# A token shift's move of 127 partitions, issued as one of 112 and one of 15

## Chip, core and metric

The kernel runs on one core of one Trainium2 chip. The metric is the device time of one execution in microseconds (us). A core has a tensor engine (PE, with its weight loads shown apart as PEld), VectorE (DVE), ScalarE (ACT), GpSimd (POOL), the queue of SyncE (SP), from which this kernel issues all its transfers, and 16 DMA engines that move the data.

## The reference

Two transformer blocks over 256 tokens of 1024 channels. The first has a feed forward part, a mixer of two branches (an RWKV-7 recurrence and a dilated attention), and a second feed forward part; the second block has two layers of three branches each. What the change touches is the input side of the RWKV-7 branch:

```python
def token_shift(p, mu):
    prev = jnp.pad(p, ((0, 0), (1, 0), (0, 0)))[:, :-1]
    return p + (prev - p) * mu

def rwkv7_time_mix(p, mu, w0, w2, a0, a2, g2, k_k, k_a, r_k, ln_w, ln_b):
    p = token_shift(p.astype(jnp.float32), mu)
    r, k, v, wd, ad, gd = _split_last(
        p, (RWKV_WIDTH, RWKV_WIDTH, RWKV_WIDTH, DECAY_LORA, AAA_LORA, GATE_LORA))
    ...
```

Each token's projection is mixed with that of the token before it; the first token has zeros before it.

## The kernel before

Tokens lie on the 128 partitions, in two tiles of 128. A projection of 512 columns is a product (`gemm`): four loads of weights of 512 KB (two chunks of 128 rows each, `weights`, line 194), for each of them a split into a high part `wh` (ACT, line 201) and a rest `wl` (DVE, line 202), and then three matmuls for each chunk and token tile (lines 213 to 215), 48 matmuls in all. The raw weights have four buffers, the split ones three.

`shift` works on a product's two accumulators. ACT copies them side by side into `pr` (128 partitions, two tiles, n columns). Token t then lies in partition t, and its predecessor one partition above, so the predecessors are brought down by a transfer inside SBUF: line 471 moves `pr[0:127]` to `pv[1:128]`, 127 partitions of 2n numbers each. Line 472 moves one row more, the last token of the first tile to the first partition of the second, and line 470 zeroes the first row. Lines 473 to 475 on DVE form `pr + (pv - pr) * mu`.

`shift` is called seven times: once with 288 columns for the low-rank inputs (`rwkv_lora`; the tiles are named `lp` and `lv` there), and six times with 512 columns, for k, r and v of each of two groups of eight heads (`rwkv_keys`). The first four are emitted one after the other; the three of the second group stand among the steps of the recurrence, the dilated attention, the gates and the rows of the modulation (products `ada` with weights `wa`, line 1103, loaded by line 1099). The string `PLAN` gives that order by hand, a letter a step. Each engine works off its own queue in order: what stands behind line 473 on DVE, as the next `wl`, starts after it, and what stands behind a transfer on SP is issued after it.

Of the kernel before, what the change touches and what calls it, by code (L numbers as in the profile page):

```python
# [17 lines left out]
DRAM = bass.MemoryType.DRAM  # L18

# the steps of other work emitted after each step of the RWKV halves (see first_block)  # L20
# the order in which the RWKV part and the work beside it are emitted, a letter a step (see first_block)
PLAN = "0000rk000rrrraa0000krk0010rgr010ar01r11rgaar1r1aarra1aaa11r1a1ara11rara1r1a1aa"
P = 128
# [16 lines left out]
def shape_constants():  # L40
    """Arrays fixed by the shapes alone: permutations, masks, rotary and Fourier tables."""
    f = np.float32
    i = np.arange(P)
    parts = []
# [6 lines left out]
    same = (i[:, None] // 64) == (i[None, :] // 64)  # L51
# [45 lines left out]
    # real input: cosines of frequencies 0 to 128, sines of 1 to 127  # L97
# [6 lines left out]
class SplitT:  # L104
    """Feature-major activations as exact hi + lo float32r parts, w tokens (256 or 512) to a stream."""
# [10 lines left out]
    def toks(self, kc, t0, n):  # L116
        """n tokens from t0 on, of chunk kc."""
        self.b.need(self, t0, n)
        o = t0 % self.w
        return tuple(x[:, kc % self.m, o:o + n] for x in self.parts[t0 // self.w, kc // self.m])  # L120
# [11 lines left out]
class Builder:  # L132
# [48 lines left out]
    def weights(self, nk, segs, per=2):  # L181
        """The (k chunk, hi, lo) of a column chunk of up to 1024 / per columns, loaded and split per k chunks at a time."""
# [34 lines left out]
    def gemm(self, xT, nk, segs, toks):  # L217
        """One column chunk (<= 512 columns, from the (W, row, col, n) segments) for the given
        (token tile, first column, end column) list; accumulators come back by token tile."""
        self.aside()  # L220
        acc = {}
        for part in self.weights(nk, segs):
            self.products(acc, xT, nk, part, toks)
            self.tick(len(toks))
        return acc

    def gemm_t(self, xT, nk, segs, w):
        """The first w tokens' column chunk, 2**18 / w columns or half as many, with the result's features on the
        partitions: accumulators of one or two chunks of 128 features."""
# [5 lines left out]
        if w == xT.w == 512:  # L235
            turns = [(f, 0, [part]) for part in self.weights(nk, segs) for f in range(nf)]
        else:
            # a bank's accumulations one after the other
            parts = list(self.weights(nk, segs, 4))
            turns = [(f, t0, parts) for f in range(nf) for t0 in range(0, w, 256)]  # L240
# [16 lines left out]
    def gemm_groups(self, xT, nk, segs, groups):  # L257
        """The same with one group of token tiles after the other, each group's accumulators yielded when complete."""
        parts = list(self.weights(nk, segs))
        for toks in groups:  # L260
            acc = {}
            for part in parts:
                self.products(acc, xT, nk, part, toks)
                self.tick(len(toks))
            yield acc
        self.aside()

# [1 line left out]
    @staticmethod  # L269
    def pipeline(items, stages):  # L270
        """Emit the stages of independent items skewed, each stage one item behind the one before; a step per yield."""
# [7 lines left out]
    def rsqrt(self, m, n, name):  # L279
        """1/sqrt(m) for [P, n] positive m: bit-level first guess, three Newton steps."""  # L280
# [29 lines left out]
    def to_split(self, src, n, xT, kc, t):  # L310
        """[128 tokens, n*128] -> feature-major hi/lo at chunk kc."""
        for c in range(0, n, 4):
# [4 lines left out]
            # stay inside one part  # L317
# [15 lines left out]
    def norm_steps(self, xT, t, x, gain, shift):  # L333
        """The normalised tile, split and feature-major in xT, in three steps of which the first needs no TensorE."""
# [15 lines left out]
    def later(self, xT, t, *args):  # L350
        """Begin tile t's norm; its other steps come between the products that follow, or when its result is read."""
# [5 lines left out]
    def tick(self, n):  # L357
        """n of a tile's products with a part of the weights have been emitted."""
# [10 lines left out]
    def ffn(self, X, xT, groups, w_in, w_out, scale, gates, nxt):  # L369
        """X[t] += scale * gates[s] * (silu(h Wg) * (h Wu)) Wo, the sigmoid's half folded into scale; xT holds h.  # L370
        groups: the token tiles in the order that the input comes in and the result goes out. nxt() gives a function
        that is called with a group once its result is complete."""
# [4 lines left out]
        w = xT.w  # L377
# [44 lines left out]
    def normed(self, X, rows, w=256):  # L422
        """An empty SplitT, and the function that fills in a group of token tiles, normalised with their stream's
        (gain, shift)."""
# [7 lines left out]
    def outgoing(self, xT, nk, W, groups, res, done):  # L432
        """The last two column chunks of a residual's update, so that one group of token tiles is complete before the
        other: with two tiles to a group the weights come twice, else the second chunk goes by groups."""
# [30 lines left out]
    def shift(self, acc, n, mu, pr, pv):  # L465
        """pr [P, 2, n] <- token-shifted projection; acc the two accumulators."""
# [4 lines left out]
        nc.sync.dma_start(out=pv[1:P, :, :], in_=pr[0:P - 1, :, :])  # L471
# [37 lines left out]
    def rwkv_keys(self, xT, hh, st):  # L509
        """Eight heads' key, receptance and value projections, shifted by a token; a step of emission per yield."""  # L510
# [7 lines left out]
    def rwkv_prep(self, hh, st):  # L518
        """The operands of their recurrence; a step of emission per yield."""
# [10 lines left out]
        # low-rank decay, in-context rate and gate  # L530
# [16 lines left out]
        # running log-decay inside chunks of 64 tokens  # L547
# [23 lines left out]
        # normalised key, rate-scaled key  # L571
# [32 lines left out]
        # operands by chunk: side of the in-context rates on the chunk's own partitions, keys and values opposite  # L604
# [37 lines left out]
    def rwkv_solve(self, hh, st, yT):  # L642
        """Their recurrence over chunks of 64 tokens, group norm, bonus and gate; a step of emission per yield."""
# [11 lines left out]
        # chunk Gram matrices, transposed: rows the b and k sides, columns a | r  # L655
# [21 lines left out]
        # unit-triangular inverse: 32-blocks by forward substitution, a block's even and odd columns on two partitions  # L677
# [43 lines left out]
        # bonus  # L721
# [8 lines left out]
        def norm(t):  # L730
            """Group norm, bonus and gate of a token tile."""
# [23 lines left out]
        # per chunk: solve, and the chunk's transition and read-out matrices  # L755
# [82 lines left out]
    def dilated(self, xT):  # L838
# [18 lines left out]
        def prep(g):  # L857
# [4 lines left out]
            # per-head normalised q | k, feature-major: [2 heads x 64, (q01, q23, k01, k23), 256 tokens]  # L862
# [23 lines left out]
        def scores(it):  # L886
# [9 lines left out]
            # statistics by (query tile, head of the group, group)  # L896
# [31 lines left out]
        # weight of group g: e^(m_g - M) / sum den_g' e^(m_g' - M)  # L928
# [20 lines left out]
    def gate_chunk(self, xT, W, col, w, bias=None):  # L949
        """tanh(half the gate pre-activation) for 256 columns, features on the partitions, tanh by accumulator."""  # L950
# [12 lines left out]
    def merged(self, w):  # L963
        """The branches' sum, features on the partitions, as slices of 512: one or two chunks of 128 features."""
# [3 lines left out]
    def project(self, yT, nk, W, c0, n, w, gates, M, first):  # L968
        """M (+)= 2 sigmoid(gate) * (y @ W) on the n columns from c0; the slices' indices."""
# [12 lines left out]
    def last_projection(self, yT, nk, W, w, gates, M, first, w_out, groups, res, nxt):  # L982
        """The last branch's projection, column chunk by column chunk; then the residual's update from M @ w_out."""
# [86 lines left out]
    def ada(self, l, wide=True):  # L1070
        """Rows silu(c) @ w_ada + b_ada for the latent and the context condition, left in DRAM."""
# [41 lines left out]
    def ada_apart(self, l):  # L1113
        """The same beside the tensor engine's work, in steps: the products and the sums over a partition's rows on
        VectorE."""
# [52 lines left out]
    def mods(self, l, i, streams):  # L1168
        """(gain, shift) rows: norm_g * (1 + scale), shift."""
# [11 lines left out]
    ORDER = ((2, 3, 0, 1), (3, 2, 1, 0))  # L1181

    def ml_gates(self, xT, W, l):
# [8 lines left out]
        # gates on partitions, tokens (context first) along the row  # L1192
# [10 lines left out]
        # input and forget gates apart, a direction's heads from partition 0 and 32, the backward direction turned round  # L1203
# [10 lines left out]
        # b: running log-forget within a chunk; c = i - b; M: running maximum with the carried one  # L1214
# [31 lines left out]
        # to columns, tokens on partitions; the backward direction's turned back  # L1246
# [24 lines left out]
    def mlstm(self, xT, W, l, outs, yT):  # L1271
# [4 lines left out]
        for h in range(4):  # L1276
# [3 lines left out]
            def product(segs):  # L1280
                """The accumulators by token tile, the first head's by stream as the input comes in."""
# [93 lines left out]
            # half of 1/rms, the sigmoid's other half  # L1375
# [123 lines left out]
    def fourier(self, xT, W, outs, yT):  # L1499
# [6 lines left out]
        for c in range(2):  # L1506
# [5 lines left out]
            for s in sorted({t // 2 for t in outs}):  # L1512
                for g in range(2):
                    # over the tokens: [channel, cosine part 0..128 | sine part 1..127]
# [8 lines left out]
                    # over the channels: even part 0..128 | odd part 1..127 of the result over the token frequencies  # L1523
# [15 lines left out]
    def second_layer(self, l, X, xT, nxt):  # L1539
        """X: residual tiles; the context's are loaded late and kept in the first layer only."""  # L1540
# [47 lines left out]
    def context(self):  # L1588
        """The context's part of the first layer's input, in steps."""
# [78 lines left out]
```

## Time and profile before

| what | us |
|---|---|
| time, median of three runs | 3113.98 |
| lowest, highest run | 3113.44, 3116.66 |
| span of the profiled execution | 3110.0 |
| PE busy in the span | 2907.0 (93%) |
| DVE busy | 1774.7 (57%) |
| ACT busy | 1178.5 (38%) |

The profile is of one execution; its span runs from the first to the last instruction. Busy time is that of instructions at work, and a busy tensor engine isn't one at its peak. "Idle before" is the time that an engine stood still ahead of an instruction, with what ended it. The granted clock is given as a share of the tensor engine's full 2.4 GHz. The chain of waits is followed back from the last instruction, at each step to what released it. The shifts lie between 224 and 510 us of the span.

### The profile page before, as it was taken

What the parts mean: (1) busy time and instruction counts of PE and PEld (TensorE: products, weight loads), DVE (VectorE), ACT (ScalarE), POOL (GpSimd) and SP (SyncE); (2) the same over time, 40 slices, a digit from 0 to 9 for tenths busy, and PEclk for the clock granted to TensorE, in tenths of its full rate; (3) what the DMA queues carried; (4) which work ended last, traced back from release to release, by engine and by line L of the source; (5) the groups of instructions that cost most, each with busy time, mean ns of one, the idle gap of its engine ahead of it and who ended that gap; (6) DMA issues with size and microseconds to landing.
All of it is one profiled execution on the core that took longest, in us unless ns stands there. A gap on an engine that the chain in (4) does not pass through costs nothing.

```text
span 3110.0 us, 42442 instructions
## 1 busy us (share of the span) xinstructions
PE 2907.0 (93%) x16704; PEld 2435.7 (78%) x16704; DVE 1774.7 (57%) x3036; ACT 1178.5 (38%) x1943; POOL 98.6 (3%) x265
## 2 busy tenths in 40 slices
PE   8994668999899999999999999999999999999998
PEld 7983445667689788898788897878778898789797
DVE  5552563755565545534767337686865455675665
ACT  4442222233344434322553333323244443454443
POOL 1010000000010000000000002000020000000000
PEclk9997787998999999999999999999999999999999
DMA  6653453553655422123124235455542234245564
GB/s 201 189 153 97 142 156 111 155 164 120 199 179 184 135 68 68 55 85 101 48 62 153 75 104 187 145 171 153 161 157 75 89 111 136 81 127 160 178 188 144
DMA packets 291231, 409.57 MB, mean 132 GB/s; under 512 B 30547, under 2 KB 181971, under 8 KB 291032
## 3 DMA queue, kind: packets, MB, share of 16 engines
q1 hardware_dynamic: 291032, 406.86, 42.8%
q8 instruction: 131, 2.15, 0.3%
q14 instruction: 68, 0.56, 0.1%
HBM read 396.98 MB, written 3.24 MB: 129 GB/s over the span
## 4 chain that ended last, share of the span: by engine, by line
PE 77%; DVE 8%; DMA 7%; issue 3%; ACT 3%; POOL 2%; SPq 0%; ACTq 0%; POOLq 0%; DVEq 0%
PE g L214 11%; PE g L215 11%; PE g L213 11%; PE g L250 10%; PE g L248 10%; PE g L249 10%; DMA pv<-pr 2%; DVE wl L202 2%; PE dC L1361 1%; PE tr L316 1%; DMA wa<-in_w_ada_dram 1%; PE ada L1103 1%; DMA wr<-in_w_in_dram 1%; PE I L1337 1%; ACT dae L1458 1%
## 5 line engine op out<-in xcount | busy, mean ns | idle before, releaser
L202 DVE TENSOR_TENSOR wl<-wr,wh 128x1024 fp32r<-128x1024 f32 (+1 forms) x606 | 733.8, 1213 | 718.3 <-ACT wh L201 716.8
L201 ACT CAST wh<-wr 128x1024 fp32r<-128x1024 f32 (+1 forms) x606 | 630.5, 1042 | 1121.6 <-PE g L215 515.1
L214 PE MATMUL g<-wl,xh 128*128 128x512 f32 (+2 forms) x1880 | 736.5, 392 | 32.5 <-DVE wl L202 32.4
L213 PE MATMUL g<-wh,xh 128*128 128x512 f32 (+2 forms) x1880 | 734.9, 394 | 17.5 <-ACT wh L201 12.8
L215 PE MATMUL g<-wh,xl 128*128 128x512 f32 (+2 forms) x1880 | 730.2, 389 | 0.0
L248 PE MATMUL g<-xh,wh 128*128 128x256 f32 (+1 forms) x2352 | 725.4, 309 | 3.6 <-ACT wh L201 3.6
L250 PE MATMUL g<-xh,wl 128*128 128x256 f32 (+1 forms) x2352 | 722.2, 307 | 1.9 <-DVE wl L202 1.9
L249 PE MATMUL g<-xl,wh 128*128 128x256 f32 (+1 forms) x2352 | 721.8, 307 | 0.1
L248 PEld LDWEIGHTS g<-xh,wh 128*128 128x128 f32 x2352 | 451.9, 192 | 32.9 <-issue 4.9
L250 PEld LDWEIGHTS g<-xh,wl 128*128 128x128 f32 x2352 | 451.5, 192 | 31.1 <-issue 7.6
L249 PEld LDWEIGHTS g<-xl,wh 128*128 128x128 f32 x2352 | 451.8, 192 | 26.6 <-issue 7.0
L214 PEld LDWEIGHTS g<-wl,xh 128*128 128x128 f32 x1880 | 361.6, 192 | 111.5 <-DVE wl L202 40.0
L213 PEld LDWEIGHTS g<-wh,xh 128*128 128x128 f32 x1880 | 359.5, 192 | 100.0 <-ACT wh L201 16.8
L215 PEld LDWEIGHTS g<-wh,xl 128*128 128x128 f32 x1880 | 361.1, 192 | 72.8 <-issue 2.9
L1153 DVE SCALAR_TENSOR_TENSOR aa<-wa,cond,aa 128x512 f32<-128x512 f32 x168 | 114.9, 745 | 3.4 <-DMA wa<-in_w_ada_dram 3.4
L303 ACT CAST xh<-tr 128x256 fp32r<-128x256 f32 (+1 forms) x114 | 50.4, 463 | 130.1 <-PE tr L316 116.9
L1103 PE MATMUL ada<-wa,cond 128*2 128x512 f32 x192 | 51.9, 643 | 46.5 <-DMA wa<-in_w_ada_dram 46.3
L1458 ACT ACTIVATE dae<-sc,dast 128x512 f32<-128x512 f32 (+1 forms) x96 | 58.5, 614 | 42.2 <-DVE dast L1456 37.3
L473 DVE TENSOR_TENSOR pv<-pv,pr 128x1024 f32<-128x1024 f32 x6 | 7.4, 1226 | 112.7 <-DMA pv<-pr 112.7
L304 DVE TENSOR_TENSOR xl<-tr,xh 128x256 fp32r<-128x256 f32 (+1 forms) x114 | 57.6, 531 | 21.7 <-ACT xh L303 21.4
L1456 DVE TENSOR_REDUCE dast<-sc 128x1 f32<-128x512 f32 (+1 forms) x96 | 53.8, 596 | 24.1 <-PE sc L1455 23.7
L316 PE MATMUL tr<-ident,hn 128*128 128x128 f32 x160 | 28.3, 312 | 39.1 <-DVE hn L343 19.5
(392 smaller groups left out, 2665.8 us busy)
## 6 DMA issues: line engine op xcount, KB each, us to landing
wr<-in_w_in_dram SPq DMA_DIRECT2D x156, 512.0 KB
wr<-in_ffn_w_in_dram SPq DMA_DIRECT2D x88, 512.0 KB
wr<-in_w_ffn_in_dram SPq DMA_DIRECT2D x84, 512.0 KB
wr<-in_w_in_dram SPq DMA_DIRECT2D x156, 256.0 KB
wr<-in_w_ffn_out_dram SPq DMA_DIRECT2D x50, 512.0 KB
wa<-in_w_ada_dram SPq DMA_DIRECT2D x48, 512.0 KB
wa<-in_w_ada_dram SPq DMA_DIRECT2D x96, 256.0 KB
wr<-in_ffn_w_out_dram SPq DMA_DIRECT2D x44, 512.0 KB
```

Source lines behind the costliest of these rows:

```text
L201: nc.scalar.copy(out=wh[:, :kn, :ntot], in_=src)
L202: nc.vector.tensor_tensor(out=wl[:, :kn, :ntot], in0=src, in1=wh[:, :kn, :ntot].bitcast(F32), op=ALU.subtract)
L213: nc.tensor.matmul(o_, xh, wh[:, n0:n1], start=(kc == 0), stop=False)
L214: nc.tensor.matmul(o_, xh, wl[:, n0:n1], start=False, stop=False)
L215: nc.tensor.matmul(o_, xl, wh[:, n0:n1], start=False, stop=(kc == nk - 1))
L248: nc.tensor.matmul(o_, wh[:, fs], xh, start=(kc == 0), stop=False)
L249: nc.tensor.matmul(o_, wh[:, fs], xl, start=False, stop=False)
L250: nc.tensor.matmul(o_, wl[:, fs], xh, start=False, stop=(kc == nk - 1))
L316: self.nc.tensor.transpose(p[:, j * P:(j + 1) * P], src[:, (c + j) * P:(c + j + 1) * P], self.ident)
L1103: nc.tensor.matmul(p[32 * j:32 * j + 2, :], self.cond[:, k, :], raws[j], start=False, stop=(k == KD - 1))
L1153: nc.vector.scalar_tensor_tensor(out=y, in0=raw, scalar=self.cond[:, k, s:s + 1], in1=acc[s], op0=ALU.mult, op1=ALU.add)
L1458: nc.scalar.activation(out=em, in_=ps[:, 0:n], func=AF.Exp, bias=st[:, m:m + 1], scale=1.0, accum_out=st[:, 2 + m:3 + m])
```

## The change

The transfer of line 471 is issued as two, of which the first has 112 partitions and the second 15. All seven calls of `shift` are changed by it. The same bytes reach the same places. The rest of the diff removes comments and leaves empty lines in their place.

```diff
         nc.gpsimd.memset(pv[0:1, 0, :], 0.0)
-        nc.sync.dma_start(out=pv[1:P, :, :], in_=pr[0:P - 1, :, :])
+
+        nc.sync.dma_start(out=pv[1:113, :, :], in_=pr[0:112, :, :])
+        nc.sync.dma_start(out=pv[113:P, :, :], in_=pr[112:P - 1, :, :])
         nc.sync.dma_start(out=pv[0:1, 1, :], in_=pr[P - 1:P, 0, :])
```

## Rows read from the trace of the kernel before

**Rows 1.** Page, busy tenths of PE in 40 slices of the span (77.75 us each).

```profile
PE   8994668999899999999999999999999999999998
```

**Rows 2.** Busy time by stretch: start:end, length, engines' busy us, clock, DMA share, GB/s.

```profile
224.00:520.00 296.00, 186.74 (x1013) 133.53 (x1013) 129.63 (x227) 70.52 (x110) 2.58 (x5) 0.77 0.41 123
...
364.00:431.00 67.00, 41.55 (x214) 27.56 (x212) 42.10 (x119) 12.81 (x16) 1.55 (x3) 0.80 0.55 171
...
330.00:372.00 42.00, 34.44 (x193) 26.66 (x194) 39.03 (x61) 15.01 (x23) 0.51 (x1) 0.84 0.39 112
```

**Rows 3.** Chain of waits, 200 to 520 us: shares; then start, length, what.

```profile
by line: DMA pv<-pr 23.9%; DMA wa<-in_w_ada_dram 9.0%; DMA kkr<-in_rwkv_k_k_dram 7.5%; DMA wr<-in_w_in_dram 7.2%; PE g L214 5.6%; PE g L215 5.3%; PE g L213 5.2%; DMA lv<-lp 4.9%; issue 4.4%; DVE wl L202 2.7%; DVE fsp L693 1.9%; SPq L615 1.8
...
225.44 15.78 DMA lv<-lp
...
255.44 22.93 DMA wr<-in_w_in_dram
...
344.21 0.23 PE g L213
...
483.25 23.48 DMA pv<-pr
```

**Rows 4.** Line 473 on DVE: what ended its idle time (us, times).

```profile
  DMA pv<-pr: 112.7, 6
  DMA lv<-lp: 12.0, 1
```

**Rows 5.** Busy time by stretch, as Rows 2: a move alone twice, many transfers once.

```profile
376.00:386.00 10.00, 0.00 (x0) 0.00 (x0) 0.00 (x0) 0.00 (x0) 0.00 (x0) 0.60 0.70 224
279.00:285.00 6.00, 6.00 (x21) 4.75 (x20) 4.76 (x5) 1.05 (x1) 0.00 (x0) 0.72 0.06 23
...
484.00:490.00 6.00, 6.00 (x31) 5.07 (x30) 1.88 (x3) 0.54 (x2) 0.00 (x0) 0.76 0.06 23
```

**Rows 6.** Transfers issued, with their count and size.

```profile
pv<-pr SPq DMA_DIRECT2D x6, 508.0 KB
...
lv<-lp SPq DMA_DIRECT2D x1, 285.8 KB
```

**Rows 7.** 346 to 352 us: GB/s in 40 slices; issues of 64-partition moves (ns, starts).

```profile
GB/s 0 0 0 34 109 75 55 177 314 382 389 417 410 287 205 219 246 205 273 246 232 178 246 246 219 82 0 0 0 82 89 123 137 218 355 335 260 130 21 0
...
L610 SPq DMA_DIRECT2D WV<-pr x4: 542/585/594, 346.0 to 347.9; - x4
```

**Rows 8.** PE's instructions after its longest idle times [idle before, what ended it].

```profile
244.13 0.42 PE L499 MATMUL lt<-ident,lp 128*64 128x128 f32 x1 [12.20 <-ACT lp L488]
...
278.23 0.80 PE L214 MATMUL g<-wl,xh 128*128 128x512 f32 x1 [16.78 <-DVE wl L202]
307.28 2.08 PE L554 MATMUL pl<-th,kbase 128*128 128x512 f32 x2 [12.72 <-ACT th L542]
...
332.39 0.79 PE L213 MATMUL g<-wh,xh 128*128 128x512 f32 x1 [11.28 <-ACT wh L201]
338.10 0.79 PE L214 MATMUL g<-wl,xh 128*128 128x512 f32 x1 [4.92 <-DVE wl L202]
...
394.45 1.87 PE L1103 MATMUL ada<-wa,cond 128*2 128x512 f32 x4 [20.27 <-DMA wa<-in_w_ada_dram]
...
409.39 0.58 PE L214 MATMUL g<-wl,xh 128*128 128x256 f32 x1 [4.13 <-DVE wl L202]
...
473.10 1.88 PE L1103 MATMUL ada<-wa,cond 128*2 128x512 f32 x4 [19.64 <-DMA wa<-in_w_ada_dram]
...
515.15 1.87 PE L1103 MATMUL ada<-wa,cond 128*2 128x512 f32 x2 [5.57 <-DMA wa<-in_w_ada_dram]
```

**Rows 9.** SP's queue: a move's issue (ns), and SP's own waits (us, times, longest).

```profile
L471 SPq DMA_DIRECT2D pv<-pr x6: 639/652/659, 251.0 to 482.2; - x6
...
SPq L1099 <- DMA pv<-pr: 16.4, 2, 8.7
SPq L194 <- DMA pv<-pr: 12.2, 2, 8.4
```

## Prediction, made before the result was seen

> **What bounds the kernel now.** I read the page's busy row first: the tensor engine is at nine tenths nearly everywhere except in the slices from about 233 to 544 us [rows 1]. One row over 224 to 520 us says how bad that stretch is: of 296 us, PE is busy 186.7, DVE 129.6, the granted clock is 0.77, and DMA moves 123 GB/s [rows 2]. No engine is full, so the stretch is bound by waits. After 520 us PE is dense again; what is taken out of this stretch arrives at the end almost whole.
>
> Which wait? The chain of waits names the shift's move: "pv<-pr" is 23.9% of 200 to 520 us and "lv<-lp" 4.9% [rows 3]. There are seven moves (one of the low-rank columns, six of k, r, v for two groups of heads) and seven pieces of 16 to 27 us in the chain. Three of them carry the label of the transfer issued next to the move, as the piece that follows the first key move is called "wr" (22.93 us); each starts at a move's issue and ends at the line that reads the moved tile. VectorE's view says the same from its side: line 473 waits 112.7 us in six times and 12.0 us in one, 124.7 in all [rows 4].
>
> Why is a move of 508 KB so long? In stretches where hardly anything but a move is in flight, the mean busy share of the 16 DMA engines is 0.06, and 23 GB/s go through [rows 5]. One sixteenth is 0.0625: the move runs on one DMA engine. 508 KB at 23 GB/s are 22.6 us, 285.8 KB are 12.7 us [rows 5, 6], which is most of what the chain shows. In contrast, four moves from 64 partitions (64 x 2 KB = 128 KB each), also inside SBUF, reach 417 GB/s and are through in some 3.3 us [rows 7]. So the path is not slow; the move is not spread.
>
> The single engine does second damage. It is also one of the 16 that every weight transfer needs, so a transfer issued behind a move is complete only after it. The tensor engine's idle list shows it: twice it waits 20 us for a "wa" transfer issued behind a move [rows 8]. And SP, which issues in order, is itself held for a move's end, 12.2 us before weight loads and 16.4 us before "wa" loads [rows 9].
>
> **The change part by part.** Removed: seven moves of 127 partitions. Added: seven of 112 and seven of 15. The single row of line 472 and all arithmetic stay.
>
> Cost of the added issue: a move's issue takes SP 0.65 us [rows 9], so 7 x 0.65 = 4.6 us, mostly in SP's own slack.
>
> Cost of the 112-partition move: no row shows this count. Bounds from the nearest rows: still one engine (112/127 of 22.6 = 20 us, 127 partitions being the nearest count), or spread as the 64-partition moves are: 448 KB at some 390 GB/s (the full slices, 382 to 417) are 1.2 us [rows 7]. I take the spread one, because 112 is 16 x 7, as 64 is 16 x 4, and 127 is divisible by no number of engines. With 0.65 us of issue, about 0.5 us until bytes flow (the 64-partition moves are issued from 346.0, bytes begin at 346.45 [rows 7]) and one 512 KB weight transfer ahead in the rings (2.3 us at the 224 GB/s of [rows 5]), it lands about 5 us after issue. With four such transfers ahead it is 12 us; that is the low end of the gain.
>
> Cost of the 15-partition move: on one engine 15/127 of 22.6 = 2.7 us, spread 0.2 us. It runs beside the other; I take 0.2, since 15 rows can lie on 15 engines.
>
> The Trainium skill, "DMA: Bandwidth & Descriptors", section "Why a DMA increments its semaphore by 16 and not by 1", says that the engines used are the largest number up to 16 that divides the slowest dimension of both sides, and names 127 partitions as a case of one. The 0.06 above agrees; by it 112 would use 16 and 15 would use 15. The same page's "Rules for kernel authors" speaks against the change: two transfers to disjoint partition halves serialize, and one should be used. By that rule alone the sum would be the rival "nothing is spread" below; no row of before shows a split transfer.
>
> Now the gain, by the tensor engine's idle pieces [rows 8], each a stall that one move makes, with what is late next:
> - Low-rank move: 12.2 us. The move landed at 241.2 [rows 3] and PE went on at 244.1, 2.9 later; with a landing near 230 it goes on near 233 to 234, and it ran dry at 231.9. Gain 10.
> - k: 16.8. PE has a whole product of 48 matmuls at 0.23 (11 us) [rows 3] to do meanwhile, so all of it goes. Gain 17.
> - r: 12.7, ended by an activation queued behind a weight load that SP issued late. Gain 12.
> - v: 11.3 + 4.9. VectorE's dense preparation (39.0 of 42 us [rows 2]) just starts earlier. Gain 15.
> - k of the second group: 20.3 + 4.1. The move lands while VectorE still transposes, so its wait there goes; but PE then wants eight "wa" transfers of 512 KB, 19 us at 224 GB/s. Gain 19.
> - r of the second group: 19.6. "wa" lands some 4 us after issue. Gain 18.
> - v of the second group: 5.6. PE was working at the low clock during this move, that stays. Gain 5.
>
> Sum 96. Clock: the 6 us after the second stall (279 to 285) run at a mean clock of 0.72 [rows 5], that is, partly at 1.2 GHz after the idle time, which loses 6 x 0.28 = 1.7 us. Six long stalls, six such tails: 10 us back. Against it, the loads must now come faster. A product's 2.1 MB of weights, 256 KB of mu and 0.5 MB of move in 11 us are 262 GB/s, against the 224 of [rows 5]: 2 us each for three products; and the 11.5 MB of 364 to 431 us (67 us at 171 GB/s [rows 2]) want 51 us, not 47. Minus 10. Net gain 96.
>
> The profiled span is 3110.0 us, 4.0 below the median of 3113.98, so I subtract from the median: 3113.98 - 96 = **3018 us**.
>
> Ends: with 12 us per landing the stalls of the low-rank move, v and r of the second group each return by 7, r's by 4, and 2 in the last: 96 - 27 = 69, or 3045 us. With no paced loads and no rest of a stall, the nine idle pieces (107.5) and 10 of clock: 117.5, or 2996; VectorE's 124.7 us of waits as the outer bound gives 2989.
>
> **The rivals.**
> 1. The loads take more of it back. SP's order and the four weight buffers were paced by waits; without them weights or "wa" arrive late, or VectorE's serial lines become the end. For it: 0.55 of DMA busy at 171 GB/s from 364 to 431 us already. Against it: over the whole stretch 36.4 MB in 200 us are only 182 GB/s. Gain 40 to 69: 3045 to 3074 us.
> 2. Nothing is spread: the change doesn't do what it says, the 112 stay on one engine with the 15 behind them. The same bytes on the same engine and 4.6 us of issues: 3118 us, no measurable difference. Only the 127-partition rows speak for it; the 64-partition rows speak against.
> 3. Slower: unspread, and the additional transfer in flight uses up one of the issues that SP can make before it is held for a move's end [rows 9]. Then one 512 KB load fewer runs ahead at each move, 2.3 us x 7 = 16, with 4.6 of issues: 3134 us. Place: SP's queue directly behind each move. It decides only where the 112-partition move saves less than 0.65 + 2.3 = 3 us of its 22.6, that is, where it is on one engine.
> 4. Only the 15 stay on one engine: 2.5 us later landing in the four moves that are not fully covered, 10 us less: 3028, inside the range.
>
> **How the numbers follow.** Forecast and rival 4 together 0.81; a gain above the outer bound 0.03; rival 1 0.11; rival 2 0.03; rival 3 0.02. The range reaches from the outer bound, 2989, into the first rival's near edge, 3047. Faster by over 0.2% (6.2 us, about what a measurement of this kernel can tell from no change): 0.95; within: 0.03; slower: 0.02.
>
> **What would show it.** Right: line 473's wait falls from 124.7 us in all to under 30; the issue of line 472 or of weight loads is no longer held for "pv<-pr"; the stretch 224 to 520 us shrinks to about 200 us with a clock near 0.9; the mean DMA share while a move is in flight is far above 0.06; the "wa" waits of 20 us fall to a few. Wrong: 0.06 stretches that remain (rivals 2, 3), or pieces of weight loads of over 5 us each in the chain (rival 1). The forecast falls if the stall moves to a queue that I took as having slack: SP's issue order, or VectorE between 372 and 431 us.

## The result

The changed kernel takes 3000.82 us (median of four runs, 2999.31 to 3002.09), the kernel before 3115.32 in the same comparison: a ratio of 0.9631, with a 95% interval of 0.9615 to 0.9647. That is 114.5 us less, where 96 were forecast (3018 us). All ratios are of fast executions; one execution of the tile-by-tile kernel, at 10591 us, is left out. The profiled execution has a span of 2997.5 us, 112.5 less than before.

### The profile after

The page's busy row of the tensor engine, against [rows 1]: the gap in the fourth to seventh slice is closed.

```profile
PE   8999999998999999999999999999999999999998
```

The stretch of the shifts, as [rows 2]: it ends at 405 in place of 520 us. Columns: start:end, length, busy us of PE, PEld, DVE, ACT and POOL with their instructions, clock, DMA share, GB/s.

```profile
224.00:405.00 181.00, 169.38 (x1033) 125.65 (x1032) 130.78 (x228) 71.21 (x112) 2.58 (x5) 0.94 0.67 203
```

The work is nearly the same (130 and 131 us of DVE, 1013 and 1033 matmuls), but the tensor engine stands idle for 181 - 169.4 = 11.6 us of it, where it was 296 - 186.7 = 109.3. Its busy time is shorter too, by 17.4 us, at a mean clock of 0.94 in place of 0.77.

The whole span splits the same way, without a choice of ends. The page after has

```profile
PE 2890.7 (96%) x16704; PEld 2429.5 (81%) x16704; DVE 1775.0 (59%) x3036; ACT 1178.6 (39%) x1943; POOL 98.4 (3%) x265
```

The tensor engine's busy time fell from 2907.0 to 2890.7, by 16.3 us, and its idle time (span less busy) from 203.0 to 106.8, by 96.2.

The line that reads the moved tile is 475 now. Its idle time, as [rows 4]:

```profile
  DMA pv<-pr: 6.7, 3
  DMA lv<-lp: 2.0, 1
```

124.7 us have become 8.7. The chain of waits over 200 to 405 us, as [rows 3], has the tensor engine's matmuls at its head and two moves among its longest pieces:

```profile
by line: PE g L214 12.7%; PE g L215 12.3%; PE g L213 11.8%; issue 5.8%; DVE wl L202 4.9%; DVE T L697 3.5%; DMA pv<-pr 3.4%; DVE fsp L695 3.2%; PE pz L543 2.6%; PE pa L546 2.5%; DMA lv<-lp 2.4%; PE pf L817 2.3%; PE pl L556 2.1%; PE tr L626 1
...
226.24 4.87 DMA lv<-lp
302.58 7.00 DMA pv<-pr
```

What is left of the tensor engine's longest idle times, as [rows 8]: nothing above 3 us.

```profile
234.99 0.30 PE L501 MATMUL lt<-ident,lp 128*64 128x128 f32 x1 [1.30 <-ACT lp L490]
...
270.04 0.73 PE L213 MATMUL g<-wh,xh 128*128 128x512 f32 x2 [2.24 <-ACT wh L201]
272.71 0.79 PE L214 MATMUL g<-wl,xh 128*128 128x512 f32 x1 [1.93 <-DVE wl L202]
...
307.15 1.03 PE L1105 MATMUL ada<-wa,cond 128*2 128x512 f32 x4 [0.69 <-DMA wa<-in_w_ada_dram]
...
325.69 0.58 PE L214 MATMUL g<-wl,xh 128*128 128x256 f32 x1 [2.75 <-DVE wl L202]
```

And the DMA engines in three stretches in which a move and weight loads go side by side, where [rows 5] had a share of 0.06 and 23 GB/s with the move alone (columns as above):

```profile
302.00:310.00 8.00, 7.31 (x50) 4.22 (x50) 7.59 (x15) 0.62 (x1) 0.00 (x0) 1.00 0.98 284
226.00:231.00 5.00, 5.00 (x23) 4.14 (x23) 2.00 (x2) 2.00 (x2) 0.00 (x0) 1.00 0.94 263
240.00:246.00 6.00, 6.00 (x28) 4.95 (x28) 4.03 (x4) 2.42 (x3) 0.00 (x0) 1.00 0.91 277
```

### Where the time came from, move by move

ACT's second copy into `pr` ends a product. Of the kernel before, for the products k, v of the first group and k, r, v of the second:

```profile
250.38 0.59 ACT L469 COPY pr<-g 128x512 f32<-128x512 f32 x1 [0.80 <-PE g L215]
...
291.16 0.58 ACT L469 COPY pr<-g 128x512 f32<-128x512 f32 x1 [0.77 <-PE g L215]
361.08 1.10 ACT L469 COPY pr<-g 128x512 f32<-128x512 f32 x2
...
446.86 0.59 ACT L469 COPY pr<-g 128x512 f32<-128x512 f32 x1 [0.65 <-PE g L215]
...
481.62 0.58 ACT L469 COPY pr<-g 128x512 f32<-128x512 f32 x1 [0.77 <-PE g L215]
```

The same copies after:

```profile
238.06 0.60 ACT L469 COPY pr<-g 128x512 f32<-128x512 f32 x1
...
259.29 0.58 ACT L469 COPY pr<-g 128x512 f32<-128x512 f32 x1 [0.77 <-PE g L215]
296.14 1.11 ACT L469 COPY pr<-g 128x512 f32<-128x512 f32 x2
...
362.75 0.59 ACT L469 COPY pr<-g 128x512 f32<-128x512 f32 x1 [0.77 <-PE g L215]
...
376.06 0.59 ACT L469 COPY pr<-g 128x512 f32<-128x512 f32 x1
```

The distance grows from 12.3 to 31.9, 64.9, 84.1 and 105.6 us. Behind the last move, at one of ACT's copies into `WV`, it is 117.4 (before, then after):

```profile
521.53 0.37 ACT L781 COPY WV<-p 64x256 f32<-64x256 f32 x1 [0.48 <-DVE WV L781]
```

```profile
404.15 0.37 ACT L783 COPY WV<-p 64x256 f32<-64x256 f32 x1 [0.48 <-DVE WV L783]
```

At the end of the span it is 112.5: 4.9 us are given back behind the stretch, why is open. The differences are what the moves ahead of each point brought; idle time, clock and paced loads are all in them:

| move | predicted, by idle time alone, us | came, us |
|---|---|---|
| low-rank | 10 | 12.3 |
| k | 17 | 19.6 |
| r and v | 12 + 15 | 33.0 |
| k, second group | 19 | 19.2 |
| r, second group | 18 | 21.5 |
| v, second group | 5 | 11.8 |
| given back behind the stretch | | -4.9 |

### The profile page after: what moved, and what is told of

Same layout as the page of the kernel before. It is cut to its first block, busy times and chain, and to the rows that moved or that the text cites. A ratio compares the mean times of both kernels' runs of the same rounds, so it can differ in the third digit from the quotient of the medians.

```text
span 2997.5 us, 42457 instructions
## 1 busy us (share of the span) xinstructions
PE 2890.7 (96%) x16704; PEld 2429.5 (81%) x16704; DVE 1775.0 (59%) x3036; ACT 1178.6 (39%) x1943; POOL 98.4 (3%) x265
## 4 chain that ended last, share of the span: by engine, by line
PE 82%; DVE 8%; issue 3%; ACT 3%; POOL 2%; DMA 2%; SPq 0%; ACTq 0%; POOLq 0%; DVEq 0%
PE g L214 12%; PE g L215 11%; PE g L213 11%; PE g L248 10%; PE g L250 10%; PE g L249 10%; DVE wl L202 2%; PE dC L1363 2%; PE tr L316 1%; PE ada L1105 1%; PE I L1339 1%; ACT dae L1460 1%; PE pf L817 1%; PE f L1530 1%; PE pf L819 1%
## 5 line engine op out<-in xcount | busy, mean ns | idle before, releaser
L213 PEld LDWEIGHTS g<-wh,xh 128*128 128x128 f32 x1880 | 357.1, 191 | 88.3 <-ACT wh L201 9.7
L316 PEld LDWEIGHTS tr<-ident,hn 128*128 128x128 f32 x160 | 22.4, 163 | 47.6 <-DVE hn L343 20.6
L330 POOL TENSOR_SCALAR rn_s<-rn_s 128x1 f32<-128x1 f32 x20 | 11.2, 560 | 1209.8 <-ACT junk L329 849.0
```

The costliest lines, as they stand in the source:

```text
L213: nc.tensor.matmul(o_, xh, wh[:, n0:n1], start=(kc == 0), stop=False)
L316: self.nc.tensor.transpose(p[:, j * P:(j + 1) * P], src[:, (c + j) * P:(c + j + 1) * P], self.ident)
```

## The experiments

Each was timed beside the kernel before. The theory: a move of 127 partitions runs on one DMA engine, 112 over many, and one engine that is held also holds the weight loads. The rivals: any cut in two does it; the new order of the instructions does it; only VectorE's own wait matters.

### One row further: 113 and 14

```diff
-        nc.sync.dma_start(out=pv[1:113, :, :], in_=pr[0:112, :, :])
-        nc.sync.dma_start(out=pv[113:P, :, :], in_=pr[112:P - 1, :, :])
+        nc.sync.dma_start(out=pv[1:114, :, :], in_=pr[0:113, :, :])
+        nc.sync.dma_start(out=pv[114:P, :, :], in_=pr[113:P - 1, :, :])
```

> The move is cut one row later: 113 and 14 partitions instead of 112 and 15, still two transfers, and every engine's instructions stand in the same order as in the changed kernel. Theory (113 is prime and stays on one DMA engine, 112 goes over 16): each move takes 113/127 of the 22.6 us that it took before, some 20 us, so at most 7 x 2.5 = 17 us of the 114 us gain remain: 3095 to 3115 us, and a DMA share of 0.06 while a move is alone. Rival A (two transfers in place of one, or the other order of instructions, make the gain): 3001 us as the changed kernel.

Measured: 3094.8 us, a ratio of 0.9941 (0.9925 to 0.9958). One row more in the first transfer takes back 97 of the 115 us. The waits of VectorE's line 475 are nearly those of [rows 4] again, and the stretch has most of its idle time back, 91.5 us (columns as above):

```profile
  DMA pv<-pr: 98.5, 6
  DMA lv<-lp: 10.9, 1
```

```profile
224.00:500.00 276.00, 184.47 (x1046) 132.32 (x1045) 131.67 (x229) 73.02 (x114) 2.58 (x5) 0.80 0.45 136
```

While a move is alone in flight, one engine of the 16 is busy again:

```profile
466.00:472.00 6.00, 6.00 (x39) 5.12 (x38) 2.62 (x5) 1.68 (x3) 0.00 (x0) 0.97 0.06 18
```

The instructions on every engine stand in the same order as in the changed kernel. That matters, because the change brought a new order with it: in the stretch, the instructions of PE, DVE, ACT and SP don't stand as in the kernel before. (There, products `p` of line 775 start at 516.95 us, between the second and the third of eight `ada` matmuls; after the change all eight stand together behind them.) With the new order and 113 rows, 18 us of the gain are left, and the 14 rows fewer on the engine were expected to give up to 17. So neither the order nor the number of transfers makes the gain. The count of partitions does.

### Halves: 64 and 63

The cut is at row 64 in place of 112.

> The move is cut in halves, 64 and 63 partitions. Theory (as many engines as divide the count): 64 rows go over 16 engines, 63 over 9 with 7 rows each, as many rows to an engine as 112 over 16 give; it lands 1 to 2 us later than the changed kernel's: 3000 to 3008 us. Rival B (a count that is not a multiple of 16 stays on one engine): 63 rows take 63/127 of 22.6 = 11.2 us, and the time is 3020 to 3050 us. Rival C (halves are served one after the other at the old pace): 3115 us.

Measured: 3004.3 us, a ratio of 0.9648 (0.9634 to 0.9663), as the theory expects and within the noise of the whole change. 63 is no multiple of 16 and is spread nevertheless (rival B wanted 3020 or more), and halves are not served at the old pace (rival C).

### A smaller one-engine part: 31 and 67 rows

The cut is at row 96 (the rest of 31) and at row 60 (the rest of 67), both remainders prime.

> The move is cut into 96 and 31 partitions. Theory: 96 rows go over 16 engines, 31 (a prime above 16) over one, in 31/127 of 22.6 = 5.5 us. The move lands some 4 us later than in the changed kernel. Covered where the tensor engine has a product to do meanwhile (k, r of the first group, k of the second), not covered in the other four: 4 x 1 to 4 us lost, 3005 to 3018 us. Rival (any cut into two parts brings the whole gain): 3001 us.

> The move is cut into 60 and 67 partitions. Theory: 60 rows go over 15 engines, 67 (prime) over one in 67/127 of 22.6 = 11.9 us, and loads issued behind it are complete only after it. The low-rank move, v and r of the second group lose 6 to 8 us each, the others 0 to 4: 3022 to 3045 us, where the prediction put its 12 us landing (3045). Rival (cover of 11 us is enough for all but the first move): 3008 to 3015 us.

Measured: 3025.2 us, a ratio of 0.9709 (0.9675 to 0.9743), and 3059.8 us, 0.9813 (0.9783 to 0.9844). With 67 rows the loss is more than expected; with 31 rows the median is, while the interval (3012 to 3034 us) still touches the expected range. The expectations of 3005 to 3018 and 3022 to 3045 rested on cover, that is, on moves during which the tensor engine has other work. By ACT's copies, taken as above but against the changed kernel, 31 rows cost 1.6 us at the first group's k, which is nearly covered, but 5.3 at the second group's k, which was expected to be, and 7.2 at its r. The idle times of the tensor engine with 31 rows show the same; among the releasers is a weight transfer that no shift reads:

```profile
236.91 0.42 PE L501 MATMUL lt<-ident,lp 128*64 128x128 f32 x1 [3.32 <-ACT lp L490]
...
278.81 1.22 PE L213 MATMUL g<-wh,xh 128*128 128x512 f32 x2 [6.10 <-ACT wh L201]
283.71 0.79 PE L214 MATMUL g<-wl,xh 128*128 128x512 f32 x1 [3.67 <-DVE wl L202]
...
326.49 1.87 PE L1105 MATMUL ada<-wa,cond 128*2 128x512 f32 x4 [3.89 <-DMA wa<-in_w_ada_dram]
...
391.89 1.87 PE L1105 MATMUL ada<-wa,cond 128*2 128x512 f32 x4 [4.75 <-DMA wa<-in_w_ada_dram]
```

Put together, with the one-engine time of seven moves worked out from 23 GB/s [rows 5] and the loss from the ratios (less 0.9631, times 3113):

| rows on one engine | one-engine us, seven moves | loss against the change, us | loss per us |
|---|---|---|---|
| 31 | 36 | 24 | 0.67 |
| 67 | 78 | 57 | 0.72 |
| 113 | 132 | 97 | 0.73 |
| 127 | 148 | 115 | 0.77 |

The loss is close to proportional. The first row is the least sure: its 24 us are uncertain by some 12, by the intervals of the two ratios. Down to 31 rows, 5.5 us a move, no one-engine part was free; shorter ones were not tried.

The pages also let one count the engines. Between kernels that move the same bytes, the number of packets differs only among those under 512 B. Before, after, and with halves:

```profile
DMA packets 291231, 409.57 MB, mean 132 GB/s; under 512 B 30547, under 2 KB 181971, under 8 KB 291032
```

```profile
DMA packets 291441, 409.57 MB, mean 137 GB/s; under 512 B 30757, under 2 KB 182181, under 8 KB 291242
```

```profile
DMA packets 291399, 409.57 MB, mean 137 GB/s; under 512 B 30715, under 2 KB 182139, under 8 KB 291200
```

Against the kernel before, these are 210 and 168 packets more, 30 and 24 for each of the seven moves; the cuts at 113, 96 and 60 have 14, 16 and 15 more for each. All five numbers come out if a transfer leaves one small packet for each engine that it uses, and uses as many engines as the largest number up to 16 that divides its rows: 1 for 127, against 16 + 15 for 112 and 15, 16 + 9 for 64 and 63, 1 + 14 for 113 and 14, 16 + 1 for 96 and 31, 15 + 1 for 60 and 67. That a small packet stands for an engine is read from this fit; nothing else shows it.

### The first four, or the last three

```diff
+        self.shifts = getattr(self, "shifts", 0) + 1
+        if self.shifts <= 4:
             nc.sync.dma_start(out=pv[1:113, :, :], in_=pr[0:112, :, :])
             nc.sync.dma_start(out=pv[113:P, :, :], in_=pr[112:P - 1, :, :])
+        else:
+            nc.sync.dma_start(out=pv[1:P, :, :], in_=pr[0:P - 1, :, :])
```

The other kernel has `> 4`.

> Only the first four moves (the low-rank columns and k, r, v of the first group of heads) are cut into 112 and 15, the last three stay whole. By the sum of the prediction the first four bring 10 + 17 + 12 + 15 = 54 us and some 7 of clock less 6 of paced loads: 3060 us. By the copies of the products in the changed kernel's trace they bring 12.8 + 19.0 + 33.1 = 65 us: 3050 us. Rival (one stretch sets the time, the other is hidden): near 3001 or near 3115 us.

> Only the last three moves (k, r, v of the second group of heads) are cut, the first four stay whole. By the sum of the prediction these bring 19 + 18 + 5 = 42 us and some 3 of clock less 4 of paced loads: 3074 us. By the copies of the products in the changed kernel's trace they bring 19.2 + 21.5 + 6.9 = 47.6 us: 3067 us. If the moves act apart from one another, the gains of this kernel and of the one with only the first four cut add up to the 114.5 us of the whole change; if they share a limit, they add up to more or less.

Measured: 3053.5 us, a ratio of 0.9803 (0.978 to 0.9825), and 3066.1 us, 0.9846 (0.9832 to 0.9861). Gains of 61 and 48 us (ratios times 3113), 109 together, against 115 for the whole change; the intervals (some 7 and 5 us to each side) cover the difference. The moves act apart from each other, and each group brings what its copies in the trace say. With the first four cut, the stalls of the last three are there as in [rows 8], 60 to 64 us earlier:

```profile
330.74 1.87 PE L1109 MATMUL ada<-wa,cond 128*2 128x512 f32 x4 [20.50 <-DMA wa<-in_w_ada_dram]
...
412.88 1.87 PE L1109 MATMUL ada<-wa,cond 128*2 128x512 f32 x4 [19.04 <-DMA wa<-in_w_ada_dram]
```

### A transfer on one engine that nothing waits for

```diff
         nc.sync.dma_start(out=pv[0:1, 1, :], in_=pr[P - 1:P, 0, :])
+        self.spares = getattr(self, "spares", 0) + 1
+        spare = self.dp.tile([P - 1, 2 * n], F32, name=f"spare{self.spares}")
+        nc.sync.dma_start(out=spare, in_=self.kb[0:P - 1, 0:2 * n])
```

> The changed kernel, and behind each of its seven moves one more transfer of 127 partitions (the same bytes as the move, from constants to scratch memory) that nothing waits for. It tells the two ways apart in which a move on one engine costs time. If the shift's own wait on VectorE is all that matters: 7 issues of 0.65 us, 3001 to 3010 us. If a transfer on one engine also holds up the weight loads, the next moves and SP's issues behind it: the tensor engine starves again for weights, most of the gain goes, 3060 to 3115 us.

Measured: 3113.4 us, a ratio of 0.9992 (0.9978 to 1.0007): the whole gain is gone, though the moves are cut. The expectation had the place wrong. The source is a constant, so nothing ties the spares to the shifts, and all seven stand in SP's queue between 20 and 139 us, in the first feed forward part. There they cost it. The first 224 us of the changed kernel, and of this one (columns as above; the first move is issued at 333.5 us here, at 224.6 in the changed kernel):

```profile
0.00:224.00 224.00, 206.04 (x1313) 187.68 (x1314) 125.77 (x142) 96.74 (x114) 16.23 (x50) 0.98 0.61 182
```

```profile
0.00:224.00 224.00, 115.72 (x640) 101.89 (x641) 63.09 (x72) 49.12 (x59) 8.52 (x28) 0.77 0.37 116
```

ACT waits for weights there, and the tensor engine with it:

```profile
57.79 1.04 ACT L201 CAST wh<-wr 128x1024 fp32r<-128x1024 f32 x1 [25.86 <-DMA wr<-in_ffn_w_in_dram]
```

```profile
58.89 0.80 PE L213 MATMUL g<-wh,xh 128*128 128x512 f32 x1 [20.37 <-ACT wh L201]
...
83.23 1.11 PE L316 MATMUL tr<-ident,th 128*128 128x128 f32 x4 [18.38 <-DVE th L393]
```

From the ratios, 0.9992 less 0.9631 are 112 us, 16 for each transfer and 0.76 for each us of the 148 on one engine, as in the table above. It is a place without any shift; what was thought to be the second damage is enough for the whole cost by itself.

### The control: 112 rows to the spare

Each spare has 112 rows in place of 127, in the same places of every queue.

> As the kernel with seven spare transfers, in the same places of every queue (they depend on nothing late and so were issued in the first feed forward part, 20 to 139 us), but each of 112 partitions in place of 127. Theory (the 127-partition spare costs its 112 us by holding one DMA engine, which every weight load needs): spread over 16 engines it costs its bytes only, 0.46 MB at some 220 GB/s, at most 2 us each: 3001 to 3015 us. Rival (seven more transfers in that stage cost it whatever their spread, by their issues or their bytes): near 3113 us.

Measured: 2998.9 us, a ratio of 0.9632 (0.9609 to 0.9655). Seven more transfers of 0.26 to 0.46 MB cost nothing that can be measured. So it is neither their issues nor their bytes; it is the one engine.

### Another queue

The 127-row spares are issued from ACT's queue in place of SP's (`nc.scalar.dma_start`), in the second kernel the whole move of the kernel before is.

> As the kernel with seven spare transfers of 127 partitions, but they are issued from ACT's queue, not from SP's. Theory A (a weight load waits because it stands behind the spare in the order of SP's own queue on that engine): from another queue the loads pass it, at half that engine's pace while it lasts; a fifth of the 112 us or less remains, 3005 to 3025 us. Theory B (the engine itself is taken, whatever queue the transfer comes from): 3090 to 3115 us.

> The kernel before, its move whole, but issued from ACT's queue. It leaves the shift's own wait on VectorE (the move still takes one engine, 23 us or more) and takes the move out of the weight loads' way. If holding up the loads is what costs, as the spare transfers say (16 us each), most of the gain comes without any cut: 3010 to 3040 us. If the wait of VectorE, behind which the next weights' split stands in its queue, is enough by itself to starve the tensor engine: 3080 to 3115 us.

Measured: 3108.3 us, a ratio of 0.9975 (0.9963 to 0.9988), and 3131.1 us, 1.0047 (1.0032 to 1.0063): another queue doesn't help, and for the move itself it is slower, by some 15 us. With the spares on ACT's queue, weight loads from SP still come late, but ACT stands still at its own issues too, so this run doesn't tell how much each costs:

```profile
74.11 1.04 ACT L201 CAST wh<-wr 128x1024 fp32r<-128x1024 f32 x1 [17.47 <-DMA wr<-in_ffn_w_in_dram]
...
98.72 23.28 ACTq L477 DMA_DIRECT2D spare<-kbase  x1
122.12 1.04 ACT L201 CAST wh<-wr 128x1024 fp32r<-128x1024 f32 x1 [22.38 <-issue]
...
158.19 1.04 ACT L201 CAST wh<-wr 128x1024 fp32r<-128x1024 f32 x1 [15.32 <-DMA wr<-in_ffn_w_in_dram]
```

With the move on ACT's queue, the tensor engine's waits for "wa" fall from some 20 us each to 4.7 at most, but the shift's own wait grows from 124.7 to 145.3:

```profile
  DMA pv<-pr: 129.8, 6
  DMA lv<-lp: 15.5, 1
```

In the chain of waits (start, length, what) the moves have become longer, four of 30 to 35 us against 23 to 27 before:

```profile
253.97 29.66 DMA pv<-pr
...
485.88 34.98 DMA pv<-pr
```

So the shift's own wait has grown while the waits for `wa` shrank, and VectorE's queue stands behind it. The times expected if the order of SP's queue is what holds the loads (3005 to 3025 us for the spares, 3010 to 3040 for the move) didn't come. But the two runs are no clean test of that guess: by the profile SP itself stood still for the end of the other queue's transfers before it issued its loads, 37.9 us for spares (first line), and 88.3 us for moves (the other three), where it was 28.6 [rows 9].

```profile
SPq L194 <- DMA spare<-kbase: 37.9, 3, 22.6
```

```profile
SPq L1099 <- DMA pv<-pr: 35.4, 2, 24.4
SPq L194 <- DMA pv<-pr: 29.1, 3, 16.7
SPq L178 <- DMA pv<-pr: 23.8, 1, 23.8
```

The kernel with the move on ACT's queue has its instructions in another order than the kernel before, too. How the engine's time is shared between the two queues stays open.

### Tile by tile

```diff
         for t in range(2):
             nc.scalar.copy(out=pr[:, t, :], in_=acc[t][:, :n])
+            nc.sync.dma_start(out=pv[1:113, t, :], in_=pr[0:112, t, :])
+            nc.sync.dma_start(out=pv[113:P, t, :], in_=pr[112:P - 1, t, :])
         nc.gpsimd.memset(pv[0:1, 0, :], 0.0)
```

> The move is issued for each of the two token tiles as soon as ACT has copied it, 112 and 15 partitions each, rows of 2 KB: four transfers in place of two. VectorE's remaining wait at the shift (8.7 us in all in the changed kernel) can shrink by what the first tile is earlier, 1.4 us a move; 14 more issues of 0.6 to 0.9 us stand in SP's queue. Theory: SP has slack there, 2996 to 3001 us. Rival: the issues hold up the weight loads behind them, 3001 to 3008 us.

> The move issued for each token tile by itself, once more with more rounds, since its first times scattered (ratio 0.9635, 0.9598 to 0.9672). If the earlier first tile is worth something beside the changed kernel's 0.9631: a ratio of 0.960 to 0.962, by the profiled spans 2992.8 against 2997.5 us. If not: 0.963 to 0.964.

Measured: ratios of 0.9635 (0.9598 to 0.9672) and 0.9628 (0.9603 to 0.9653); the change as it is has 0.9631. VectorE's wait for the moves falls from 8.7 to 1.5 us, though a wait of 6.4 us for ScalarE now stands at the same line, and the profiled span falls from 2997.5 to 2992.8. A gain of that size can't be told from the noise of the times. What was left to gain at the shift's own wait is that little.

## Why the prediction was right, point by point

**The reading of the cause held.** A share of 0.06 was one engine of 16; 113 rows against 112 show it without any other difference. The divisor rule that the Trainium skill states (page "DMA: Bandwidth & Descriptors", section "Why a DMA increments its semaphore by 16 and not by 1") fits every count tried: 113, 67, 31 and 127 behave as on one engine, 112 and the halves of 64 and 63 as spread, and the small packets come out to the engine. The advice under "Rules for kernel authors" on the same page, not to bother with two transfers to disjoint partition halves, gives as its reason that both use all 16 engines either way. For 127 rows, which use one, it doesn't hold: the measurement decides. By the small packets the 15 rows ran on 15 engines, so rival 4 didn't come true.

**One reading of the chain didn't hold.** The three pieces called `wr`, `kkr` and `wa` were read as moves under another name, each ending at the line that reads the moved tile. Line 473 read the first key move at 275.82 us, but the `wr` piece ends at 255.44 + 22.93 = 278.4; the `wa` piece ends at 473.05, where the `ada` matmul that reads the load begins [rows 8]. By their names and times these pieces are loads issued just behind a move, landing just after it. The second damage stood in the chain itself, under its right name.

**The sum of idle times held.** 96 us were to go; the tensor engine's idle time fell by 97.6 in the stretch and by 96.2 over the whole span. So close a match is partly luck: the 10 us that the loads were to take back would be idle time too, so by the prediction's own terms 86 were to go.

**Two terms were mis-sized, and their errors add.** The clock was to give back 10 us, by six tails of 1.7; the busy time fell by 16.3 over the span (17.4 in the stretch). The one tail that was measured stood for all, and they are not alike: four `ada` matmuls behind a long wait took 1.87 us [rows 8], after the change 1.03; the `pl` and `px` matmuls behind r's stall took 6.4 us (307.28 to 313.68, where the next product begins), after the change 3.4 (262.52 to 265.96). The loads were to take back 10 us at a pace of 224 GB/s; the DMA engines delivered 263 to 284 GB/s where it mattered, at a share of 0.91 to 0.98, and took back nothing to speak of. The 224 came from a stretch in which one engine was still occupied by a move, and so was no measure of all 16. 96.2 and 16.3 are the 112.5 us of the profiled span; the forecast had 96 + 10 - 10.

**The cover was wrong, though the number wasn't.** The step "k: PE has a whole product to do meanwhile, so all of it goes" and the low end (12 us landings still leave 69 us of gain, 3045) assumed that a late move costs only where its reader waits. With 67 rows on one engine, some 12 us a move, the time was 3060. What fails is the cover: the weights for the work that was to cover the move need the same engine. In that run the tensor engine waits 9.4 and 9.8 us for `wa` loads that read no moved tile, where it was 0.7 after the change. The prediction named that as second damage and then priced only landings. A landing made late by loads ahead of a spread move, which is what the low end meant, was not tried.

**Landing.** Forecast: about 5 us after issue, the issue itself included. The first of the low-rank move's two issues began at 224.60 us and the move had landed at 226.24 + 4.87 = 231.1, 6.5 us later. The longest, with the DMA share at 0.98, took 8.5 us (301.04 to 309.58).

**The rivals.** The loads didn't take it back (rival 1: SP's waits for a move fell from 28.6 to 1.5 us). Rivals 2 and 3 are what a cut at 113 looks like, and even that is faster than before by 18 us, with 14 rows fewer on the engine. What rival 3 feared is there, in that run: the second issue of a move held SP for 3.6 to 7.6 us each time, where it took 0.9 after the change. A loss from it can't be seen in the time.

## What to carry to other kernels

Look at the mean DMA share while a large transfer is in flight: a sixteenth means one engine, and its length is then bytes by some 23 GB/s, for the two sizes moved here (286 and 508 KB). Choose the partition count of a transfer, or cut it, so that both parts spread; one row more or less (113 for 112) decides. And where a busy tensor engine lives on loads, price a one-engine transfer by its length on every load that needs the engine, not by who waits for its data: here each us of it cost 0.7 to 0.8 us, even with nobody waiting for it.

## What the runs showed of the hardware that was not expected

- Seven transfers of 127 rows that nothing waits for cost 112 us in a stage with the tensor engine at nine tenths; with 112 rows they cost nothing.
- The cost is nearly proportional to the time on one engine, 0.67 to 0.77 us per us from 36 to 148 us (the first of these uncertain by half).
- The number of packets under 512 B on the page tells how many engines a transfer used: 30 more for each move that goes as 112 and 15, in place of one of 127.
- Issued from ACT's queue, the same transfers cost 107 us (0.9975 less 0.9631, times 3117). One issue held ACT for 23.3 us, where the others of such a transfer took 0.2 to 8.4.
